# The down projection's weight split by transfers: a casting load for the high part, an adding load for the low part

## The chip, the core and the metric

The kernel runs on one core of a Trainium2 chip. The metric is device time in microseconds for one launch, the median of several runs. The engines are named as the profile names them: PE is TensorE (PEld its weight loads), DVE is VectorE, ACT is ScalarE, POOL is GpSimd and SP is SyncE; SPq, ACTq and POOLq are the queues from which they issue transfers.

## The reference, cut to what matters

One decoder layer for 256 positions of width 1024: RMSNorm, attention with 16 heads and a relative-position bias, residual, RMSNorm, a gated feed-forward network (FFN) with a causal depthwise convolution of width 3, residual, and a last RMSNorm. The change lies in the FFN, whose inner width is 2816:

```
y = rms_norm(h, ffn_norm)
u = y @ w_up                         # 256 x 1024 @ 1024 x 5632
u = causal depthwise conv of width 3 (u) + conv_b
gate, val = split(u)
h = h + (silu(gate) * val) @ w_down  # 256 x 2816 @ 2816 x 1024
out = rms_norm(h, final_norm)
```

All of it is float32.

## The kernel before

**Products from parts.** TensorE multiplies in the type fp32r, which keeps fewer bits than float32. Each operand is therefore split in two: a high part, which is the value rounded to fp32r, and a low part, which is the value less its high part. A product is the sum of three matmuls: high by high, low (activations) by high (weights), high by low.

**Splitting the weights.** Weights come from memory in loads of 1 MB into one of four `raw` tiles (`load`, L80, issued from SP's queue at L100). They are cut into units of 128 x 1024 numbers. For each unit ACT copies the raw numbers to a tile `whi` of fp32r, which rounds them (`split_hi`, L144), and DVE subtracts that from the raw numbers into a tile `wlo` (`split_lo`, L157; three units at a time of the attention part are subtracted by POOL). Behind the subtraction that ends a load's use, the next load is issued (`load_next`). There are 11 `whi` tiles and 10 `wlo` tiles in rotation.

**Order.** The list `groups` (L113 to L119) gives the order of the units, two to a group: value, query and key, output projection ("o"), and then the FFN: 22 groups "up", one for each 128 columns of the gate and the matching 128 of the value, with the 11 groups "d" of w_down (256 rows each) among them, one behind every second "up", the last three at the end (`TAIL`). `unit` (L161) makes one high part and one low part, with the high parts one unit ahead of the low parts; `split_to(g, ahead)` (L169) makes units until those of group `g` and `ahead` more are made. The program is written by hand in this order; each engine works off its own list in order.

**The FFN.** For each j of 22, `up(j)` makes 48 matmuls of 256 columns into a `bank` of PSUM; `gates(j)` (L645) evacuates it on DVE (`u`, L649), makes the convolution on ACT and DVE (`cv`, L653 to L665), the SiLU on ACT (`sl`, L672) and, one j late, the gated product and its high and low parts `at` (L656 to L668), with two calls of `unit` between these steps. Then units are split ahead, 6 or (from j = 8) 8 units beyond group j (L702). After every second j from 3 on, `down(i)` (L674) adds two units' products to four accumulators: for each unit four high matmuls of 512 columns and two low ones for each half of the positions (`rows_product`, L309). The last three groups are multiplied at the end, the first 128 positions first, and each half of the positions is normalised and stored by `finish` (L727): a power on POOL (L732), the scaling on DVE and ACT from `xg` to `o` (L737, L739), and the stores.

The start of the FFN has one more power on POOL, that of the second RMSNorm (`rstds`, L240), and the load of the last norm's weights, `gf` (L618), is issued from POOL's queue.

Of the kernel before, what the change touches and what calls it, by code (L numbers as in the profile page):

```python
# [8 lines left out]
F32 = mybir.dt.float32  # L9
F32R = mybir.dt.float32r  # L10
BF16 = mybir.dt.bfloat16
AF = mybir.ActivationFunctionType
ALU = mybir.AluOpType

P = 128
S = 256
NT = S // P
D = 1024
# [13 lines left out]
UNITS = 10  # L32
RAWS = 4
AHEAD = 6
WARM = 6
MORE_WARM = 2

# [10 lines left out]
def tile_block(ctx: ExitStack, tc, x, attn_norm, w_qkv, w_o, rel_bias, ffn_norm, w_up, conv_w,  # L48
               conv_b, w_down, final_norm, out):
    nc = tc.nc  # L50
# [3 lines left out]
    wraw = ctx.enter_context(tc.tile_pool(name="wraw", bufs=RAWS))  # L54
    wsp = ctx.enter_context(tc.tile_pool(name="wsp", bufs=UNITS))
# [21 lines left out]
    wq, wo, wu, wd = w_qkv[0], w_o[0], w_up[0], w_down[0]  # L77
# [25 lines left out]
    def parts(g):  # L103

        kind, i = g
        if kind in ("v", "o", "d"):
            t = raws[kind, i].rearrange("p (k c) -> p k c", k=2)
            return [t[:, 0, :], t[:, 1, :]]
        pair = ("qc", "kc") if kind == "qk" else ("gc", "uc")
        j = i % 2  # L110
        return [raws[n, i // 2].rearrange("p (k c) -> p k c", k=KD)[:, :, j * P:(j + 1) * P] for n in pair]

    groups = [("v", i) for i in range(4)] + [("qk", p) for p in range(NP)] + [("o", i) for i in range(4)]  # L113
# [5 lines left out]
    groups += [("d", i) for i in range(first_tail, NG)]  # L119
    order = []  # L120
    for kind, i in groups:
        if kind in ("v", "o", "d"):
            order.append((kind, i))
        elif i % 2 == 0:
            order += [(n, i // 2) for n in (("qc", "kc") if kind == "qk" else ("gc", "uc"))]
    place = {g: n for n, g in enumerate(groups)}
    hi, lo = {}, {}
    state = {"hi": 0, "lo": 0, "load": 0, "by": nc.vector}

    def load_next():  # L130
        if state["load"] < len(order):
            load(order[state["load"]])
            state["load"] += 1

    def split_hi():
        n, u = divmod(state["hi"], 2)
        if n >= len(groups):
            return
        state["hi"] += 1
        g = groups[n]  # L140
        src = parts(g)[u]
        hi[g, u] = wsp.tile([P, 1024], F32R, name="whi", bufs=UNITS + 1)
        h = hi[g, u].rearrange("p (k c) -> p k c", k=KD) if len(src.shape) == 3 else hi[g, u]
        nc.scalar.activation(h, src, AF.Copy)  # L144

    def split_lo():
        n, u = divmod(state["lo"], 2)
        if state["lo"] == state["hi"]:
            return
        state["lo"] += 1  # L150
        g = groups[n]
        src = parts(g)[u]
        lo[g, u] = wsp.tile([P, 1024], F32R, name="wlo", bufs=UNITS)
        h, l = hi[g, u].bitcast(F32), lo[g, u]
        if len(src.shape) == 3:
            h, l = (a.rearrange("p (k c) -> p k c", k=KD) for a in (h, l))
        state["by"].tensor_tensor(l, src, h, op=ALU.subtract)  # L157
        if u if g[0] in ("v", "o", "d") else g[1] % 2:
            load_next()

    def unit(count=1):  # L161

        for _ in range(count):
            if state["hi"] == state["lo"]:
                split_hi()
            split_hi()
            split_lo()

    def split_to(g, ahead=0):  # L169
        n = 2 * (place[g] + 1) + ahead  # L170
        unit(max(0, n - state["lo"]))
# [30 lines left out]
    for name, src in (("g2", ffn_norm[0]), ("b", conv_b[0]), ("w0", conv_w[0, 0]), ("w1", conv_w[0, 1]),  # L202
                      ("w2", conv_w[0, 2])):
        i, r = ROWS[name]
        n = src.shape[0] // P
# [11 lines left out]
    def first_params():  # L217
        ps = bank()
        nc.tensor.transpose(ps[:, :KD], row1, ident[:KD, :KD])
        nc.scalar.activation(g1, ps[:, :KD], AF.Copy, scale=math.sqrt(D))  # L220
# [56 lines left out]
    def keep_warm(n):  # L277
        for _ in range(n):
            mm(warm[:, :P], ones, ones, True, True)

    keep_warm(WARM)
    first_params()
# [5 lines left out]
    while d1 >= 0:  # L288
# [4 lines left out]
        n = d1 - d0 + 1  # L293
# [38 lines left out]
    g = ("v", 0)  # L332
# [37 lines left out]
    for i in range(4):  # L370
# [4 lines left out]
        for kk in range(2):  # L375
            k = 2 * i + kk
# [237 lines left out]


    fp = ctx.enter_context(tc.tile_pool(name="fp", bufs=1))
    gf = fp.tile([P, D], F32, name="gf")
    nc.gpsimd.dma_start(gf, bass.AP(tensor=final_norm.tensor, offset=final_norm.offset, ap=[[0, P], [1, D]]))  # L618
    at = {}
# [3 lines left out]
    def taps(col):  # L623
        return tuple(params[:, i, r + col:r + col + 1] for i, r in (ROWS[n] for n in ("w0", "w1", "w2", "b")))
# [12 lines left out]
    def up(j):  # L637
        split_to(("up", j))
        ps = up_ps()
        up_k(j, ps, range(KD))  # L640
        gates(j, ps)
# [3 lines left out]
    def gates(j, ps):  # L645

        if j < NF:
            u = fp.tile([P, 2, S], F32, name="u", bufs=2)
            nc.vector.tensor_tensor(u, ps, rb2.unsqueeze(1).to_broadcast([P, 2, S]), op=ALU.mult)  # L649
            c = cv[j] = fp.tile([P, 2, S], F32, name="cv", bufs=2)  # L650
            for a in range(2):
                w0, w1, w2, b = taps(a * NF + j)
                nc.scalar.activation(c[:, a, :], u[:, a, :], AF.Identity, scale=w2, bias=b)  # L653
        if j > 0:
            s = sl[j - 1]
            nc.vector.tensor_tensor(s, s, cv[j - 1][:, 1, :], op=ALU.mult)  # L656
            at[j - 1] = fp.tile([P, 2, S], F32R, name="at", bufs=10)
            nc.scalar.activation(at[j - 1][:, 0, :], s, AF.Copy)
        unit()
        if j < NF:  # L660
            for a in range(2):
                w0, w1, w2, b = taps(a * NF + j)
                nc.vector.scalar_tensor_tensor(c[:, a, 1:], u[:, a, :S - 1], w1, c[:, a, 1:],  # L663
                                               op0=ALU.mult, op1=ALU.add)
                nc.vector.scalar_tensor_tensor(c[:, a, 2:], u[:, a, :S - 2], w0, c[:, a, 2:],  # L665
                                               op0=ALU.mult, op1=ALU.add)
        if j > 0:
            nc.vector.tensor_tensor(at[j - 1][:, 1, :], s, at[j - 1][:, 0, :].bitcast(F32), op=ALU.subtract)  # L668
        unit()
        if j < NF:  # L670
            sl[j] = fp.tile([P, S], F32, name="sl", bufs=2)
            nc.scalar.activation(sl[j], c[:, 0, :], AF.Silu)  # L672

    def down(i, chains, whole=False):  # L674
        split_to(("d", i))
        for c in chains:
            if c not in accs:
                accs[c] = acc()
        for kk in range(2):
            k = 2 * i + kk  # L680
            rows_product(accs, at[k], ("d", i), kk, chains, k == 0,
                         k == NF - 1 or (CHAINS[3] if whole and kk else False), kk == 1 and chains == CHAINS)
# [12 lines left out]
    for j in range(NF):  # L695
        if j < 2:
            gates(j, first[j])
        else:
            up(j)
        if j == 4:  # L700
            nc.scalar.activation(gf, gf, AF.Copy, scale=math.sqrt(D))
        split_to(("up", j), AHEAD if j < 8 else AHEAD + 2)  # L702
        i = (j - 3) // 2
        if j >= 3 and j % 2 == 1 and i < first_tail:
            down(i, CHAINS, i == first_tail - 1)
            split_to(("d", i), AHEAD if j < 8 else AHEAD + 2)

    gates(NF, None)

    xg = [fp.tile([P, D], F32, name=f"xg{t}") for t in range(NT)]
    ends = {t: fp.tile([P, 4], F32, name=f"ends{t}") for t in range(NT)}

    def weighted(t, c, y):
        nc.vector.tensor_tensor(xg[t][:, c], y, gf[:, c], op=ALU.mult)

    def square(t, c, n, y):
        nc.scalar.activation(junk[t][:, c], y, AF.Square, accum_out=ends[t][:, n:n + 1])  # L719
# [7 lines left out]
    def finish(t, n):  # L727

        square(t, LAST[t], n, last[t])
        r = small.tile([P, 1], F32, name="rf")  # L730
        nc.vector.scalar_tensor_tensor(r, ends[t][:, n:n + 1], D * EPS, ends[t][:, 3:4], op0=ALU.add, op1=ALU.add)  # L731
        nc.gpsimd.tensor_tensor(r, r, minus_half, op=ALU.pow)  # L732
        weighted(t, LAST[t], last[t])
        o = fp.tile([P, D], F32, name="o", bufs=2)
        rows = out[0, t * P:(t + 1) * P, :]
        for c in QUARTERS:
            nc.vector.tensor_scalar(o[:, c], xg[t][:, c], r, None, op0=ALU.mult)  # L737
            nc.sync.dma_start(rows[:, c], o[:, c])
        nc.scalar.activation(o[:, :512], xg[t][:, :512], AF.Copy, scale=r)  # L739
        nc.scalar.dma_start(rows[:, :512], o[:, :512])  # L740
# [18 lines left out]
    down(NG - 1, [(0, 1)])  # L759
    last[0] = add_part(0, right, accs[0, 1])  # L760
    finish(0, 0)
    for i in range(first_tail, NG):
        down(i, [(1, 0)])
# [43 lines left out]
```

## Time and profile before

| what | value |
|---|---|
| median of 3 runs | 298.86 us (298.61 to 301.47) |
| the profiled execution's span, first to last instruction | 298.1 us |
| outside the span (median less span) | 0.8 us |
| busy in the span: PE, DVE, ACT, POOL | 290.8, 229.1, 170.4, 35.1 us |
| granted clock of PE, mean | 0.998 |
| moved by transfers | 62.07 MB, mean 208 GB/s |
| of it from POOL's queue (q0, software) | 2.65 MB |
| the FFN on PE, first full up product to the last chain's end | about 120 to 292 us |

How to read it: the engines run beside each other, so their busy times don't add up to the span; what counts is which engine the others wait for, and that is read from the waits and from the chain that ended last. A group's row gives line, engine and operation, output and inputs with shapes, count, then busy time and the mean of one in ns, then the idle time of the engine just before. In the timeline each row has start, length and what ran; the bracket at its end is the idle time before it and what ended that. "us to landing" of a transfer runs from its issue until all of it has arrived.

### The profile page before, as it was taken

The numbers are of one execution on the slowest core, as the hardware profiler recorded it, in microseconds if no ns is written. First come the engines' busy times: TensorE is split into PE (matmuls) and PEld (weight loads), VectorE is DVE, ScalarE is ACT, GpSimd is POOL, SyncE is SP. The second block draws the span as 40 slices with busy tenths as digits, with TensorE's granted clock in tenths as the row PEclk, the third lists the DMA queues.
The fourth block names the chain that finished last, engine by engine and source line by source line (L and its number), as shares of the span: only waits on it lengthen the run. The fifth ranks groups of instructions, "written<-read, shape, count | busy, mean of one in ns | idle before, by whom it ended". The sixth has DMA issues, their size and how long they took to land.

```text
span 298.1 us, 5455 instructions
## 1 busy us (share of the span) xinstructions
PE 290.8 (98%) x2112; PEld 268.7 (90%) x2112; DVE 229.1 (77%) x426; ACT 170.4 (57%) x309; POOL 35.1 (12%) x61
## 2 busy tenths in 40 slices
PE   8999999999999999999999999999999999999992
PEld 7888999979978789998989899999989898999882
DVE  3864978479588586899895959998795959599752
ACT  4684749149165676477582727766474727275341
POOL 4605008319100003000000000000000000000010
PEclk9999999999999999999999999999999999999999
DMA  7999497698796964364938191976364747400011
GB/s 243 417 384 342 155 329 211 177 412 214 253 370 166 324 214 152 125 237 144 343 122 303 44 354 49 324 224 244 132 216 136 257 143 281 144 0 2 0 70 70
DMA packets 44245, 62.07 MB, mean 208 GB/s; under 512 B 1772, under 2 KB 37308, under 8 KB 44220
## 3 DMA queue, kind: packets, MB, share of 16 engines
q1 hardware_dynamic: 42492, 58.17, 57.8%
q0 software_dynamic: 848, 2.65, 2.7%
q10 hardware_dynamic: 880, 0.92, 1.1%
q8 instruction: 16, 0.26, 0.4%
q14 instruction: 9, 0.07, 0.1%
HBM read 57.90 MB, written 3.83 MB: 207 GB/s over the span
## 4 chain that ended last, share of the span: by engine, by line
PE 86%; DMA 5%; DVE 3%; issue 3%; ACT 0%; SPq 0%; POOL 0%; POOLq 0%; DVEq 0%
PE bank L73 41%; PE acc L73 37%; PE spare L73 5%; DMA raw<-in_w_o_dram 3%; DMA weights<-turned 1%; DMA turned<-weights 1%; DVE weights L477 1%; DVE weights L475 1%; PE bank L254 1%; PE acc L254 1%; DVE xs L724 0%; DVE wlo L157 0%; SPq L482 0%; POOL rf L732 0%; ACT junk L719 0%
## 5 line engine op out<-in xcount | busy, mean ns | idle before, releaser
L73 PE MATMUL bank<-yt,whi 128*128 128x256 f32 x704 | 120.6, 277 | 0.0
L157 DVE TENSOR_TENSOR wlo<-raw,whi 128x1024 fp32r<-128x1024 f32 x90 | 107.2, 1219 | 2.0 <-ACT whi L144 1.1
L73 PEld LDWEIGHTS bank<-yt,whi 128*128 128x128 f32 x704 | 106.2, 188 | 0.0
L144 ACT ACTIVATE whi<-raw 128x1024 fp32r<-128x1024 f32 x96 | 95.3, 1047 | 9.7 <-DMA raw<-in_w_qkv_dram 6.0
L73 PE MATMUL bank<-yt,wlo 128*128 128x256 f32 x352 | 97.2, 276 | 0.0
L73 PEld LDWEIGHTS bank<-yt,wlo 128*128 128x128 f32 x352 | 66.1, 188 | 0.0
L653 ACT ACTIVATE cv<-u,params 128x256 f32<-128x256 f32 x44 | 24.1, 594 | 65.5 <-DVE u L649 65.5
L73 PE MATMUL acc<-whi,at 128*128 128x512 f32 x164 | 44.8, 390 | 0.0
L73 PEld LDWEIGHTS acc<-whi,at 128*128 128x128 f32 x164 | 30.1, 188 | 5.8
L649 DVE TENSOR_TENSOR u<-bank,rb 128x512 f32<-128x512 f32 x22 | 15.2, 691 | 21.1 <-PE bank L73 21.1
L73 PE MATMUL acc<-yt,whi 128*128 128x256 f32 x160 | 27.8, 278 | 0.0
L73 PE MATMUL acc<-wlo,at 128*128 128x512 f32 (+1 forms) x90 | 26.1, 370 | 0.0
L73 PEld LDWEIGHTS acc<-yt,whi 128*128 128x128 f32 x160 | 24.2, 188 | 0.0
L665 DVE SCALAR_TENSOR_TENSOR cv<-u,params,cv 128x254 f32<-128x254 f32 x44 | 21.3, 483 | 1.6
L73 PE MATMUL acc<-yt,wlo 128*128 128x256 f32 x80 | 22.2, 278 | 0.0
L732 POOL TENSOR_TENSOR rf<-rf,minus_half 128x1 f32<-128x1 f32 x2 | 1.5, 740 | 172.4 <-DVE rf L731 172.4
L663 DVE SCALAR_TENSOR_TENSOR cv<-u,params,cv 128x255 f32<-128x255 f32 x44 | 21.0, 478 | 0.3 <-ACT cv L653 0.3
L73 PE MATMUL acc<-whi,ot 128*128 128x512 f32 x64 | 20.1, 396 | 0.0
L73 PEld LDWEIGHTS acc<-wlo,at 128*128 128x128 f32 x90 | 16.9, 188 | 3.5
L73 PE MATMUL acc<-whi,yt 128*128 128x512 f32 x64 | 17.9, 404 | 0.0
L464 ACT ACTIVATE weights<-weights,nz 128x128 f32<-128x128 f32 (+1 forms) x32 | 14.1, 442 | 5.6 <-DVE nz L460 5.6
L73 PE MATMUL spare<-yt,whi 128*128 128x256 f32 x96 | 17.0, 281 | 0.0
(118 smaller groups left out, 334.5 us busy)
## 6 DMA issues: line engine op xcount, KB each, us to landing
raw<-in_w_up_dram SPq DMA_DIRECT2D x22, 1024.0 KB, 5.2
raw<-in_w_down_dram SPq DMA_DIRECT2D x11, 1024.0 KB, 6.4
raw<-in_w_qkv_dram SPq DMA_DIRECT2D x10, 1024.0 KB, 8.5
raw<-in_w_o_dram SPq DMA_DIRECT2D x4, 1024.0 KB, 6.7
weights<-turned SPq DMA_DIRECT2D x7, 384.0 KB, 3.8
turned<-weights SPq DMA_DIRECT2D x24, 96.0 KB, 2.0
raw<-in_w_qkv_dram SPq DMA_DIRECT2D x4, 512.0 KB, 7.6
bias<-line_d POOLq DMA_DIRECT2D x8, 256.0 KB, 4.1
```

The costliest lines, as they stand in the source:

```text
L73: nc.tensor.matmul(o, lhsT, rhs, start=start, stop=stop, skip_group_check=True)
L144: nc.scalar.activation(h, src, AF.Copy)
L157: state["by"].tensor_tensor(l, src, h, op=ALU.subtract)
L254: nc.tensor.transpose(ps[:, a, t * P:(t + 1) * P], xt[t][:, (k + a) * P:(k + a + 1) * P], ident)
L464: nc.scalar.activation(sc[p][:, a, c], sc[p][:, a, c], AF.Exp, bias=nm[:, j], accum_out=z[:, j])
L475: nc.vector.tensor_tensor(w, w, rz[:, :, t:t + 1].to_broadcast([P, 2, c.stop - c.start]), op=ALU.mult)
L477: nc.vector.transpose(blocks.rearrange("p (J g i) -> p g J i", J=4, g=6), sc[p].rearrange("p a (c J i) -> p (a c) J i", c=3, J=4))
L649: nc.vector.tensor_tensor(u, ps, rb2.unsqueeze(1).to_broadcast([P, 2, S]), op=ALU.mult)
L653: nc.scalar.activation(c[:, a, :], u[:, a, :], AF.Identity, scale=w2, bias=b)
L663: nc.vector.scalar_tensor_tensor(c[:, a, 1:], u[:, a, :S - 1], w1, c[:, a, 1:], op0=ALU.mult, op1=ALU.add)
L665: nc.vector.scalar_tensor_tensor(c[:, a, 2:], u[:, a, :S - 2], w0, c[:, a, 2:], op0=ALU.mult, op1=ALU.add)
L732: nc.gpsimd.tensor_tensor(r, r, minus_half, op=ALU.pow)
```

## The change

The 22 units of w_down are no longer loaded as raw numbers.

- Their high parts come from a transfer from memory straight into a tile `dhi` of type fp32r, issued from POOL's queue; the transfer casts. `cast_ahead` issues it, up to five units (`CASTS`) ahead of the unit whose high part is next, once the FFN's pool is open. There are six `dhi` tiles (`DOWNS`).
- In the place of the ACT copy, ACT writes the negative of the high part to the unit's `wlo` tile.
- In the place of the DVE subtraction, POOL's queue issues a second transfer of the same rows of w_down, which adds them onto that tile (`accum_op=ALU.add`).
- w_down is left out of the list of SP's loads, so the four `raw` tiles are used for w_up alone in the FFN.
- To make room, `at` has 8 tiles and not 10, and `xg` and `o` of the last steps are the two halves of `raw` tiles.

```diff
+CASTS = 5
+DOWNS = 6
...
     for kind, i in groups:
-        if kind in ("v", "o", "d"):
+        if kind == "d":
+            continue
+        if kind in ("v", "o"):
             order.append((kind, i))
...
-    state = {"hi": 0, "lo": 0, "load": 0, "by": nc.vector}
+    state = {"hi": 0, "lo": 0, "load": 0, "cast": 0, "pool": None, "by": nc.vector}
+
+    def down_rows(g, u):
+        k = 2 * g[1] + u
+        return wd[k * P:(k + 1) * P, :]
+
+    def cast_ahead():
+
+        while state["pool"] is not None and state["cast"] < min(state["hi"] + CASTS, 2 * len(groups)):
+            n, u = divmod(state["cast"], 2)
+            state["cast"] += 1
+            g = groups[n]
+            if g[0] == "d":
+                hi[g, u] = state["pool"].tile([P, 1024], F32R, name="dhi", bufs=DOWNS)
+                nc.gpsimd.dma_start(hi[g, u], down_rows(g, u))
...
         n, u = divmod(state["hi"], 2)
         if n >= len(groups):
             return
+        g = groups[n]
+        cast_ahead()
         state["hi"] += 1
-        g = groups[n]
+        if g[0] == "d":
+            lo[g, u] = wsp.tile([P, 1024], F32R, name="wlo", bufs=UNITS)
+            nc.scalar.activation(lo[g, u], hi[g, u].bitcast(F32), AF.Copy, scale=-1.0)
+            return
...
         state["lo"] += 1
         g = groups[n]
+        if g[0] == "d":
+            nc.gpsimd.dma_start(lo[g, u], down_rows(g, u), accum_op=ALU.add)
+            return
...
     fp = ctx.enter_context(tc.tile_pool(name="fp", bufs=1))
+    state["pool"] = fp
...
-            at[j - 1] = fp.tile([P, 2, S], F32R, name="at", bufs=10)
+            at[j - 1] = fp.tile([P, 2, S], F32R, name="at", bufs=8)
...
-    xg = [fp.tile([P, D], F32, name=f"xg{t}") for t in range(NT)]
+    ends_of = [wraw.tile([P, 2048], F32, name="raw") for _ in range(NT)]
+    xg = [t[:, :D] for t in ends_of]
...
-        o = fp.tile([P, D], F32, name="o", bufs=2)
+        o = ends_of[t][:, D:]
```

How the order moves, at the two places that the prediction speaks of. First ACT at the beginning of the FFN, from the first of its rows at which a unit of w_down is split; a row is the line, the operation, output and input with the tile's number, and the size. Before:

```order
L144 ACTIVATE whi_1719<-raw_1551 128x1024
L144 ACTIVATE whi_1730<-raw_1561 128x1024
L672 ACTIVATE sl_1736<-cv_1713 128x256
L144 ACTIVATE whi_1767<-raw_1561 128x1024
L144 ACTIVATE whi_1771<-raw_1586 128x1024
L653 ACTIVATE cv_1828<-u_1826,params_118 128x256 x2
```

After (line numbers of the changed kernel):

```order
L167 ACTIVATE whi_1723<-raw_1350 128x1024
L162 ACTIVATE wlo_1734<-dhi_1585 128x1024
L699 ACTIVATE sl_1740<-cv_1717 128x256
L162 ACTIVATE wlo_1771<-dhi_1649 128x1024
L167 ACTIVATE whi_1776<-raw_1555 128x1024
L680 ACTIVATE cv_1830<-u_1828,params_118 128x256 x2
```

These are the units of group ("d", 1) (`raw_1561` before). Each negation stands where the copy stood; its input is now a `dhi` tile and its output a `wlo` tile.

Second, POOL's list behind the second RMSNorm's power. Before, nothing stood there up to the end of the kernel:

```order
L618 DMA gf_1407<-in_final_norm_dram 128x1024
L240 TENSOR_TENSOR rstd_1503<-rstd_1503,minus_half_116 128x2
L732 TENSOR_TENSOR rf_3398<-rf_3398,minus_half_116 128x1
L732 TENSOR_TENSOR rf_3470<-rf_3470,minus_half_116 128x1
```

After, the first of the 44 transfers that now stand between the powers:

```order
L266 TENSOR_TENSOR rstd_1503<-rstd_1503,minus_half_116 128x2
L146 DMA dhi_1509<-in_w_down_dram 128x1024
L146 DMA dhi_1511<-in_w_down_dram 128x1024
L176 DMA wlo_1561<-in_w_down_dram 128x1024
L146 DMA dhi_1585<-in_w_down_dram 128x1024
L176 DMA wlo_1577<-in_w_down_dram 128x1024
L146 DMA dhi_1649<-in_w_down_dram 128x1024
L176 DMA wlo_1734<-in_w_down_dram 128x1024
L146 DMA dhi_1774<-in_w_down_dram 128x1024
```

The rows of L146 are casting transfers and those of L176 adding ones; the casts of a group stand behind the adds of the group before it, tile by tile, and each add waits there for ACT's negation.

## Prediction

> **What bounds the kernel now.** I read the page's engine totals first, then who TensorE waited for, then the chain that ended last, then the stretches.
>
> ```profile
> PE 290.8 (98%) x2112; PEld 268.7 (90%) x2112; DVE 229.1 (77%) x426; ACT 170.4 (57%) x309; POOL 35.1 (12%) x61
> ```
>
> ```profile
> PE spare L73 <- DVE ones L199: 1.0, 1, 1.0
> PE spare L73 <- DMA weights<-turned: 0.4, 1, 0.4
> ```
>
> ```profile
> 120.42 13.64 PE bank L73 x120
> 134.07 5.46 PE acc L73 x25
> 139.53 10.90 PE bank L73 x96
> 150.43 5.46 PE acc L73 x25
> ...
> 254.05 21.78 PE bank L73 x192
> 275.83 6.83 PE acc L73 x30
> ...
> 293.76 0.72 ACT o L739
> ```
>
> ```profile
> core 0: us, PE busy (x) PEld busy (x) DVE busy (x) ACT busy (x) POOL busy (x), PEclk, DMA share, GB/s
> 140.00:260.00 120.00, 120.00 (x897) 113.62 (x897) 97.92 (x148) 69.19 (x105) 0.00 (x0) 1.00 0.62 210
> ```
>
> The second fence is all that TensorE (PE) ever waited for: 1.4 us, none of it in the part that is changed. The chain (start, length, what) is PE alone from 120.42 to 282.66: the FFN is a period of 10.90 us of up products and 5.46 us of down products, 16.36 us together, with no gap, and in the 120 us window PE is busy 120.00 at a granted clock of 1.00. VectorE (DVE) has 22 us to spare there, ACT 51 us. The matmuls stay: same shapes, same count. So the stage is worth what PE does in it, and the edit can only leave it alone or make PE wait.
>
> **What is removed.** For w_down's 22 tiles, the DVE subtractions go, and the ACT copies become ACT negations in the same places.
>
> ```profile
> L157 DVE TENSOR_TENSOR wlo<-raw,whi 128x1024 fp32r<-128x1024 f32 x90 | 107.2, 1219 | 2.0 <-ACT whi L144 1.1
> L144 ACT ACTIVATE whi<-raw 128x1024 fp32r<-128x1024 f32 x96 | 95.3, 1047 | 9.7 <-DMA raw<-in_w_qkv_dram 6.0
> ```
>
> DVE: 22 x 1.219 = 26.8 us of work less. What hides it is PE: nothing on PE waits for DVE there, so it is worth 0. ACT: 22 copies of 1.047 us out, 22 negations of the same tile size and engine in; 0. Eleven 1 MB loads leave SP's queue; w_up then has all four `raw` tiles to itself, so its loads go out earlier; 0. At the end `xg` and `o` lie in `raw` tiles whose last readers, splits of w_up, are long done when they are written; 0, and 0 too for the last steps (L716 to L740), which keep their order.
>
> **What is added: 44 transfers of 512 KB from POOL's queue.** This trace has neither a casting nor an adding transfer. The nearest rows:
>
> ```profile
> raw<-in_w_up_dram SPq DMA_DIRECT2D x22, 1024.0 KB, 5.2
> raw<-in_w_down_dram SPq DMA_DIRECT2D x11, 1024.0 KB, 6.4
> gf<-in_final_norm_dram POOLq DMA_DIRECT2D x1, 512.0 KB, 4.9
> ```
>
> `gf` has the cast's bytes, its row length (4 KB a partition) and its queue: 4.9 us from issue to landing. I take that for a cast alone; below it I see no reason to go, and the upper end is twice it, 9.8. The window above moves 210 GB/s at a share of 0.62, so full engines move 210/0.62 = 339 GB/s, and 512 KB (0.52 MB) occupies them 1.55 us; the other 3.35 us of `gf` are fixed. An adding transfer has to read what stands in the tile as well as what comes. Lower end: `gf`'s 4.9. Upper end: two such transfers, one behind the other, 9.8. I take the bytes twice with the fixed part once, 3.35 + 3.1 = 6.5 us, as w_up's row shows that doubled bytes (1 MB) land in 5.2, far nearer 4.9 than 9.8.
>
> The Trainium skill (Collectives: The Full Stack, "The bandwidth ceiling: the fold count and why AG ≠ RS ≠ AR") says that an add inside the transfer engines is slow because of its two source reads and not because of the addition, a measured factor of 1.93 between reduce and copy. No run here shows that yet; by it the moved part would be 1.55 x 1.93 = 3.0 us, an estimate from that page, and the sum below would stay as it is.
>
> POOL itself: `gf`'s issue took 0.57 us, so 44 issues are about 25 us of an engine with nothing else in the FFN.
>
> ```profile
> 111.44 0.57 POOL L618 DMA_DIRECT2D gf<-in_final_norm_dram  x1 [35.94 <-PE acc L73]
> 117.04 2.76 POOL L240 TENSOR_TENSOR rstd<-rstd,minus_half 128x2 f32<-128x2 f32 x1 [5.04 <-DVE rstd L239]
> ```
>
> **Is any of it late?** Each tile is now a chain: cast, ACT's negation, add, PE. Start with group 0, the first, whose cast stands right behind the power at 117.04 and so leaves at 119.80.
>
> ```profile
> 121.65 1.09 ACT L653 ACTIVATE cv<-u,params 128x256 f32<-128x256 f32 x2 [3.22 <-DVE u L649]
> 122.65 1.99 ACT L144 ACTIVATE whi<-raw 128x1024 fp32r<-128x1024 f32 x2
> 124.55 0.40 ACT L672 ACTIVATE sl<-cv 128x256 f32<-128x256 f32 x1
> 126.34 1.09 ACT L653 ACTIVATE cv<-u,params 128x256 f32<-128x256 f32 x2 [1.40 <-DVE u L649]
> 127.34 0.40 ACT L658 ACTIVATE at<-sl 128x256 fp32r<-128x256 f32 x1
> 127.65 1.99 ACT L144 ACTIVATE whi<-raw 128x1024 fp32r<-128x1024 f32 x2
> ...
> 138.39 1.99 ACT L144 ACTIVATE whi<-raw 128x1024 fp32r<-128x1024 f32 x2
> 140.29 0.40 ACT L672 ACTIVATE sl<-cv 128x256 f32<-128x256 f32 x1
> 140.59 2.00 ACT L144 ACTIVATE whi<-raw 128x1024 fp32r<-128x1024 f32 x2
> ```
>
> ```profile
> L73 PE MATMUL acc<-wlo,at x90: 277/389/389, 134.8 to 287.7; 128*128 128x512 f32 x74, 128*128 128x256 f32 x16
> ```
>
> By the order of ACT the negation of group 0's first tile is the second half of the pair at 122.65: it could start at 123.65, but its cast lands at 119.80 + 4.9 = 124.7. ACT stands still 1.05 us; queued behind it are the SiLU `sl` at 124.55 and `cv` at 126.34, and the 1.40 us that ACT idled before 126.34 cover it. If the cast took the 9.8, ACT would be 6 us late and `cv`, `at` and PE's next evacuation with it. The negation ends at 125.7, and PE first reads a low part of w_down at 134.8 (first start in the row above). So the first add has 134.8 - 125.7 = **9.1 us** against 6.5. The second tile's negation is the first half of the pair at 127.65, ends 128.7, and PE wants it half a down later, 134.8 + 2.73 = 137.5: **8.8 us**.
>
> Here the engines have company. From 125.7 on, before the second add can be complete, they move the first add (1.05 MB read), the next cast that stands between the two adds in POOL's queue (0.52), the second add (1.05) and the load that SP issues at about that time (1.05): 3.67 MB. At 339 GB/s that is 10.8 us, with the fixed 3.35 it lands at 139.9, **2.3 us late**. At the 426 GB/s that the row below (105 to 140 us in 40 slices) reaches, 8.6 us and 137.7, **0.2 us late**; with adds that read once, 2.62 MB, 7.7 us and 136.8, in time. The bounds are 0 and 2.3; I take **0.5**, near the row with the fuller engines.
>
> ```profile
> GB/s 8 0 37 243 407 421 328 362 378 423 327 47 33 0 0 0 0 0 19 0 0 84 277 382 376 248 417 426 187 0 0 178 362 372 281 25 0 0 0 35
> ```
>
> Group 1: negations end at 140.4 and 141.6 (second of the pair at 138.39, first of that at 140.59), PE wants them 0.75 into the down product as before (134.8 against 134.07), at 151.2, and half a down later at 153.9: 10.8 and 12.3 us. From j = 8 on the splits run two units further ahead, so the later ones have more. The last tile, group 10:
>
> ```profile
> 272.46 1.05 ACT L144 ACTIVATE whi<-raw 128x1024 fp32r<-128x1024 f32 x1
> ```
>
> Its negation ends at 273.5; PE's chain reads it last in the piece that ends at 282.66, one 0.23 us matmul (6.83/30) earlier, 282.4: **8.9 us**, with no load beside it. 6.5 fits; 0. Its cast waits for PE to be done with the tile six before it, group 7's, about 254.05: 18 us ahead of its negation; 0.
>
> Engines over a period of 16.36 us: w_up 2.10 MB, casts 1.05, adds 2.10 read: 5.25 MB at 339 GB/s = 15.5 us. Tight, but under the period.
>
> **Sum.** 298.1 span + 0.8 around it (the median 298.86 less the span) + 0 for the work removed + 0.5 at group 0 = 299.4 us.
>
> **Rivals.** *Adds that land late at the two ends (chance 0.19).* PE waits from 9.1 us issue to landing at group 0 and from 8.9 at the last tile; all between have 10.8 or more. For it: SP's loads and both kinds of POOL's transfers share the engines at group 0. Against: the last tile is alone. An add of 12 us costs 2.9 + 3.1 = 6.0 us: 304.9.
>
> The Trainium skill (DMA: Bandwidth & Descriptors, "Queues, rings and completion order") has each engine take turns between the queues that have work. What it would do here belongs to this rival: with SP's load beside it the add's 3.1 us become 6.2 and it lands in 9.6 instead of 9.1, a wait of half a microsecond; no row here separates two queues.
>
> *The transfer engines become the bound (0.16).* If the adding or the casting moves a third of the rate, adds count 3.15 MB: 6.30 MB a period, 18.6 us, 2.2 us over PE's 16.36. Eight periods: 18 us, 317. For it: nothing in the trace prices an add. Against: it takes three times the price of the same bytes.
>
> *A gain (0.03, of it 0.02 over 1%).* DVE's 26.8 us free a place where PE waits for it. Against: PE's waits above are 1.4 us in all. Even all of it would give 297.5.
>
> **Chances.** 0.62 for the forecast: PE never or hardly waits. About 1% (3 us) is what a measurement of this kernel can tell from no change; the two late cases lie beyond it, 0.35. Faster 0.02, within 1% 0.63. The range begins at 298.2, since nothing on PE is taken away, and reaches to 311, through the first rival and short of the second; the forecast's own is 298.2 to 301.8.
>
> **What would show it.** Right: PE still has its pairs of 10.90 and 5.46 us without gaps, DVE's L157 group falls from 90 to 68, and the adds land under 9 us. Wrong: waits of PE on `wlo` transfers, first at about 135 and last before 283; or, if the engines are full, w_up's landing well over 5.2 us, ACT waiting for `raw` or `dhi` and a DMA share near 1.

## The result and the profile after

The changed kernel takes 301.24 us (median of 15 runs, 300.2 to 302.2), the kernel before, on the same chip, 299.08 us (15 runs): a ratio of 1.0053, with a 95% interval of 1.0039 to 1.0068. By the ratio that is 1.6 us more (the means of the runs lie 1.5 us apart, the medians 2.2), inside the 1% within which the forecast lay, and the sign is clear. The profiled execution has a span of 299.6 us where that of before had 298.1.

First the engine totals of the changed kernel and its groups for the new work (line numbers are those of the changed kernel, 2 to 28 higher than before):

```profile
PE 289.7 (97%) x2112; PEld 267.6 (89%) x2112; DVE 205.7 (69%) x404; ACT 170.5 (57%) x309; POOL 67.4 (22%) x105
...
L183 DVE TENSOR_TENSOR wlo<-raw,whi 128x1024 fp32r<-128x1024 f32 x68 | 81.7, 1220 | 4.6 <-ACT whi L167 3.5
L176 POOL DMA_DIRECT2D wlo<-in_w_down_dram x22 | 19.7, 894 | 111.6 <-ACT sl L699 70.2
L162 ACT ACTIVATE wlo<-dhi 128x1024 fp32r<-128x1024 f32 x22 | 22.8, 1046 | 1.4 <-DMA dhi<-in_w_down_dram 1.4
L146 POOL DMA_DIRECT2D dhi<-in_w_down_dram x22 | 17.3, 838 | 14.7 <-PE acc L75 14.7
```

DVE is 23.4 us less busy (229.1 to 205.7) and PE does the same work. The 22 negations cost ACT what the copies did (1046 ns against 1047). So the work moved as planned, and the time grew.

Who PE waited for in the changed kernel (in all, times, longest):

```profile
PE acc L75 <- DMA wlo<-in_w_down_dram: 1.3, 1, 1.3
PE spare L75 <- DVE ones L225: 1.0, 1, 1.0
PE acc L75 <- DVE whi L366: 0.8, 1, 0.8
```

Only the first wait is new in the FFN; the other two lie at the kernel's start. The chain that ended last (start, length, what) shows where it stands:

```profile
113.66 5.46 PE bank L75 x48
...
127.91 9.94 DMA wlo<-in_w_down_dram
137.84 0.04 issue
137.89 2.12 PE acc L75 x9
140.00 10.90 PE bank L75 x96
150.90 5.46 PE acc L75 x25
...
276.30 6.83 PE acc L75 x30
...
294.23 0.72 ACT raw L767
```

One add, issued at 127.91 and landed 9.94 us later, is on the chain; it is the second of group 0, and behind it the pairs of 10.90 and 5.46 us run without a gap. From the first up product (113.66) to the end of the piece of 6.83 us it is 169.47 us; before, from 114.75 to 282.66, it was 167.91: **1.56 us more, all at group 0**. (The FFN starts at another time in each execution, 113.4 to 115.5 us in the profiles of this study, because the attention part in front of it, which no kernel here changes, varies; so stages are compared by their length.)

The second half of the cost stands behind the last product. From the start of ACT's last scaling to the end of the span it is 299.6 - 294.23 = 5.4 us; before, 298.1 - 293.76 = 4.3. The instructions that close the program, before and after (count, ns min/median/max, first and last start; SP's first drain stands behind its waits for the stores):

```profile
L803 SPq EVENT_SEMAPHORE  x11: 17/28/28, 295.0 to 298.1; - x11
L803 POOLq DRAIN  x3: 46/93/1582, 293.1 to 297.9; - x3
L803 SPq DRAIN  x3: 7/7/7, 297.3 to 297.6; - x3
```

```profile
L831 SPq EVENT_SEMAPHORE  x11: 17/28/28, 295.5 to 299.5; - x11
L831 POOLq DRAIN  x3: 46/98/5172, 293.6 to 299.3; - x3
L831 SPq DRAIN  x3: 7/7/7, 297.9 to 299.0; - x3
```

POOL's first drain starts together with its last power, at 293.1 and 293.6, so that some 0.6 us of its time is the power's. It took 1.58 us and was over at 294.7, long before the stores (297.3); now it takes 5.17 us and is over at 298.8, behind the stores (297.9), and the last barrier waits for it. That adds **1.0 us**, and nothing in the prediction spoke of it. In these two profiles 1.56 and 1.0 us, less the 1.1 us by which this execution's FFN started earlier (113.66 against 114.75), are the 1.5 us between the spans.

Transfers (landing is the median from issue; q0 is POOL's queue, with packets, MB and share), and the same stretch as before:

```profile
q1 hardware_dynamic: 39500, 46.63, 47.7%
q0 software_dynamic: 7184, 25.72, 34.0%
...
raw<-in_w_up_dram SPq DMA_DIRECT2D x22, 1024.0 KB, 13.4
dhi<-in_w_down_dram POOLq DMA_DIRECT2D x22, 512.0 KB, 9.2
wlo<-in_w_down_dram POOLq DMA_DIRECT2D x22, 512.0 KB, 7.4
```

```profile
140.00:260.00 120.00, 120.00 (x898) 113.62 (x897) 80.84 (x130) 68.00 (x103) 21.60 (x31) 1.00 0.92 259
```

The share rose from 0.62 to 0.92 and w_up's loads land in 13.4 us where they took 5.2, yet PE is busy 120.00 of 120 us: all of that is hidden.

### The profile page after: what moved, and what is told of

It is laid out like the page before. It is cut to its first block, busy times and chain, and to the rows that moved or that the text cites. A ratio compares the mean times of both kernels' runs of the same rounds, so it can differ in the third digit from the quotient of the medians.

```text
span 299.6 us, 5492 instructions
## 1 busy us (share of the span) xinstructions
PE 289.7 (97%) x2112; PEld 267.6 (89%) x2112; DVE 205.7 (69%) x404; ACT 170.5 (57%) x309; POOL 67.4 (22%) x105
## 4 chain that ended last, share of the span: by engine, by line
PE 86%; DMA 5%; issue 3%; DVE 2%; ACT 1%; POOL 0%; POOLq 0%; SPq 0%
PE acc L75 41%; PE bank L75 37%; PE spare L75 7%; DMA wlo<-in_w_down_dram 3%; DMA raw<-in_w_qkv_dram 1%; PE acc L280 1%; DVE u L676 0%; DVE xs L752 0%; PE bank L280 0%; DVE wlo L183 0%; ACT cv L680 0%; DVE cv L692 0%; ACT wlo L162 0%; POOL rf L760 0%; DVE cv L690 0%
## 5 line engine op out<-in xcount | busy, mean ns | idle before, releaser
L183 DVE TENSOR_TENSOR wlo<-raw,whi 128x1024 fp32r<-128x1024 f32 x68 | 81.7, 1220 | 4.6 <-ACT whi L167 3.5
L167 ACT ACTIVATE whi<-raw 128x1024 fp32r<-128x1024 f32 x74 | 74.3, 1048 | 10.8 <-DMA raw<-in_w_qkv_dram 7.0
L75 PE MATMUL acc<-dhi,at 128*128 128x512 f32 x164 | 44.8, 390 | 0.0
L176 POOL DMA_DIRECT2D wlo<-in_w_down_dram x22 | 19.7, 894 | 111.6 <-ACT sl L699 70.2
L75 PEld LDWEIGHTS acc<-dhi,at 128*128 128x128 f32 x164 | 30.1, 188 | 5.8
L162 ACT ACTIVATE wlo<-dhi 128x1024 fp32r<-128x1024 f32 x22 | 22.8, 1046 | 1.4 <-DMA dhi<-in_w_down_dram 1.4
L146 POOL DMA_DIRECT2D dhi<-in_w_down_dram x22 | 17.3, 838 | 14.7 <-PE acc L75 14.7
## 6 DMA issues: line engine op xcount, KB each, us to landing
raw<-in_w_up_dram SPq DMA_DIRECT2D x22, 1024.0 KB, 13.4
```

The costliest lines, as they stand in the source:

```text
L75: nc.tensor.matmul(o, lhsT, rhs, start=start, stop=stop, skip_group_check=True)
L146: nc.gpsimd.dma_start(hi[g, u], down_rows(g, u))
L162: nc.scalar.activation(lo[g, u], hi[g, u].bitcast(F32), AF.Copy, scale=-1.0)
L176: nc.gpsimd.dma_start(lo[g, u], down_rows(g, u), accum_op=ALU.add)
```

## The experiments

**Group 0 by DVE.** The first two tiles of w_down are split as before: they are back in the list of SP's loads, and each `g[0] == "d"` of the change becomes this:

```diff
-        if g[0] == "d":
+        if g[0] == "d" and g[1] > 0:
```

> The changed kernel, with group 0 of w_down (its first two tiles) split as before: a load by SP, a copy by ACT, a subtraction by DVE; the other ten groups by casting and adding transfers. Theory A (two small costs: the second add of group 0 lands 1.3 us late for PE, and POOL's drain at the end, 5.17 us against 1.58, holds the last barrier by about 1.0 us): PE waits for no wlo transfer, its FFN is as long as before (from the last transposes at about 114 to the end of the last chain), the drain stays at about 5.0 us; ratio to before 1.002 to 1.004. Rival B (the transfer engines are full all through the FFN and group 0 is only where it shows first): the wait moves to group 1, PE still waits about 1 us or more, ratio stays at 1.005. Rival C (the end is later because the stores now read raw tiles): cannot be told apart here.

Measured: ratio 1.0021 (1.0005 to 1.0037), with no wait for `wlo`. Its chain and its drain:

```profile
113.71 5.46 PE bank L75 x48
119.17 0.22 PE acc L272 x2
119.38 13.64 PE bank L75 x120
133.03 5.46 PE acc L75 x25
...
274.79 6.83 PE acc L75 x30
```

```profile
L831 POOLq DRAIN  x3: 46/97/4847, 292.1 to 297.5; - x3
```

113.71 to 281.62 is 167.91 us, the length of before to the hundredth. No wait appears at group 1, so rival B has nothing for it: what is late is late at group 0 alone. The drain has four transfers less and 0.325 us less, 81 ns each; from 11 transfers (rb, line, eight of bias, gf) and 1.58 us before to 55 and 5.17 it is 3.59/44 = 82 ns each.

**The last powers off POOL**, in the changed kernel, with group 0 by DVE on top, and in the kernel before as control:

```diff
     gates(NF, None)
+    nc.scalar.activation(junk[0][:, :1], ones[:, :1], AF.Sqrt)
...
-        nc.gpsimd.tensor_tensor(r, r, minus_half, op=ALU.pow)
+        nc.scalar.activation(r, r, AF.Sqrt)
+        nc.vector.reciprocal(r, r)
```

> The changed kernel, with the two last powers on POOL replaced by a square root on ACT (its table loaded early by a dummy) and a reciprocal on DVE, so that POOL's last instruction is the issue of the last add at about 274 and its drain runs beside PE's last products. Its control is the kernel before with the same replacement. Theory A: the drain is over before the stores are, the time from the last store to the end of the span is as in the control, and the difference to the control is the wait at group 0 alone, 1.3 to 1.6 us. Rival C (the stores from raw tiles are what is late): the difference to the control stays at about 2.5 us. Against the kernel before: ratio 1.002 to 1.005 by A.

> Both together: group 0 split as before by DVE, and the last powers off POOL. Theory A: nothing is left of the cost; within 0.5 us of the control (the kernel before with the same roots), PE waits for no wlo transfer. Rival B: 1 us or more above the control, with PE waiting at group 1. Rival C: 1 us above the control at the end.

> Control: the kernel before with the last two powers on POOL replaced by a square root on ACT and a reciprocal on DVE. Its drain of 1.58 us did not hold the end in the kernel before, so by A nothing is gained by its being early; what changes is the power itself, 0.55 us on POOL against some 0.4 us on ACT and DVE with one more handover: ratio 0.997 to 1.002. B and C expect the same.

Measured: 1.0004 (0.9976 to 1.0033), 0.9985 (0.9962 to 1.0008) and, for the control, 1.0008 (0.9985 to 1.0030). From the end of PE's last product to the end of the span it is 5.8 us in both changed kernels (291.98 to 297.8, 291.06 to 296.9) and 5.7 in the control (291.90 to 297.6), where the changed kernel with its powers on POOL has 6.7 (292.86 to 299.6) and the kernel before 5.7 (292.39 to 298.1). They too store from `raw` tiles, so rival C is out. With the root on ACT, POOL's drain of the changed kernel lies beside PE's last products: it starts at 273.3, when the last add is issued, takes 10.53 us with that add's landing (8.2 us) in it, and ends at 283.8. With both costs taken out the change is as fast as its control (0.9985 against 1.0008, the intervals overlap). In the profile of the first of the three, the wait at group 0 was small:

```profile
PE acc L75 <- DMA wlo<-in_w_down_dram: 0.2, 1, 0.2
```

The difference to the control that was expected there, 1.3 to 1.6 us, did not come (the intervals overlap): its add landed in 8.85 us and not 9.94. Its FFN is still 0.9 us longer than 167.91; 0.2 of that is the wait, and why PE's next pair was slower too (11.31 us for the up products, not 10.90) is open. The wait at group 0 is not the same in every execution.

**Adds as casts.**

```diff
-            nc.gpsimd.dma_start(lo[g, u], down_rows(g, u), accum_op=ALU.add)
+            nc.gpsimd.dma_start(lo[g, u], down_rows(g, u))
```

> The changed kernel with the adding transfers made plain casting ones: the same rows, size, queue and waits, but the tile is overwritten and nothing is added, so the low parts are left out of the result. It prices the adding alone. In the changed kernel 44 transfers of POOL's queue take 34.0% less 2.7% of 299.6 us, 93.8 us of full engines, 2.13 us each. Theory A (an add moves about twice the bytes, a cast the price of a plain load, 1.55 us): the share of POOL's queue falls to about 25%, the share in the window 140 to 260 from 0.92 to about 0.76, a transfer in the place of an add lands in 5 to 6 us (7.4 before), PE's wait at group 0 goes to 0 to 0.5 us, the drain stays at 5.2 us: ratio 1.001 to 1.004. Rival B (casting is as dear as adding, 2.1 us each): share, landing and wait stay as in the changed kernel, ratio 1.005.

Measured: 1.0033 (1.0011 to 1.0054). Its transfers and its stretch:

```profile
q0 software_dynamic: 7184, 25.72, 25.3%
...
wlo<-in_w_down_dram POOLq DMA_DIRECT2D x22, 512.0 KB, 5.1
```

```profile
140.00:260.00 120.00, 120.00 (x897) 113.62 (x897) 81.50 (x132) 67.69 (x103) 16.89 (x32) 1.00 0.79 263
```

As theory A had it. A cast occupies the engines (25.3% - 2.7%) x 299.2/44 = 1.54 us, the price of a plain load; an add (93.8 - 22 x 1.54)/22 = 2.73 us, 1.77 times as much. Its row on POOL is longer too, 0.89 us against 0.53 in the mean, but the next issue starts 0.56 us behind it (124.20 and 124.76 in the changed kernel). With the plain transfer in the add's place PE does not wait at group 0 (114.84 to 282.75, 167.91 us), and what is left of the cost is the drain, 5172 ns as in the changed kernel.

**The drain by itself**: the kernel before with 88 transfers of 2 KB.

```diff
         split_to(("up", j), AHEAD if j < 8 else AHEAD + 2)
+        for _ in range(4):
+            nc.gpsimd.dma_start(fp.tile([H, BUCKETS], F32, name="tiny", bufs=4), rel_bias)
```

> The kernel before with 88 more transfers of 2 KB from POOL's queue, four for each j of the FFN, into small tiles that nobody reads. It takes the drain by itself: so far POOL's last drain took 1.58 us with 11 transfers issued from its queue, 4.85 with 51 and 5.17 with 55, which is 82 ns for each. Theory A (the drain grows with the number of transfers, whatever their size): 1.58 + 88 x 0.082 = 8.8 us; it ends at about 301.9 where the stores were over at 297.3, so the span grows by about 4.5 us, ratio 1.013 to 1.017, with PE unchanged. Rival D (it grows with bytes or descriptors: a tiny transfer has 16 rows of 128 bytes where a tile has 128 of 4 KB): drain 1.6 to 2.5 us, ratio 1.000.

Measured: 1.015 (1.0121 to 1.0179), 303.55 us.

```profile
L805 SPq EVENT_SEMAPHORE  x11: 17/28/28, 294.0 to 301.6; - x11
L805 POOLq DRAIN  x3: 46/102/8767, 292.1 to 301.4; - x3
```

The drain took 8.77 us where 1.58 + 88 x 3.59/44 = 8.76 follows from the 82 ns for each, though a transfer is 2 KB and not 512; rival D is out. PE's FFN keeps its 167.91 us (113.70 to 281.61); 0.18 MB of transfers cost 4.5 us at the end.

**One and two more copies for each tile**, to find the limit of the transfer engines:

```diff
             nc.gpsimd.dma_start(lo[g, u], down_rows(g, u), accum_op=ALU.add)
+            for _ in range(1):
+                nc.sync.dma_start(dram.tile([P, D], F32, name="more", bufs=8), down_rows(g, u))
```

> The changed kernel with one more plain copy of 512 KB for each tile of w_down, from memory to memory, issued by SP behind the tile's add and read by nobody: two more per period of the FFN. It asks how much room the transfer engines have left, where the share stands at 0.92. If a share of 1 is the limit (at 1.55 us a copy): 15.05 + 3.1 = 18.15 us of engine work in a period of 16.36, so 1.8 us more for each of eight periods, about 14 us, 313 us, PE waiting for w_up or wlo all along. If the share has idle time in it (a packet's time counts its own waiting): under 4 us more than the changed kernel, waits at group 0 and the end only.

> The same with two more copies for each tile, four per period: 15.05 + 6.2 = 21.25 us of work in 16.36. If a share of 1 is the limit: 4.9 us a period, about 39 us, 340 us. If there is idle time in the share: well under 20 us more. Between this and the run with one copy, the slope prices a transfer in a full stage: 22 more of 1.55 us would be 34 us less what stays hidden.

Measured: with one copy 301.85, 304.36, 308.34 and 308.59 us in four runs, with two 329.96 us (ratio 1.1030, 1.0993 to 1.1068). First, with one copy more, who PE waited for, the stretch, and the last add in the chain; then, with two, PE's wait, ACT's splits of w_up with what they waited for, w_up's loads, and the stretch:

```profile
PE acc L75 <- DMA wlo<-in_w_down_dram: 1.5, 1, 1.5
```

```profile
140.00:260.00 120.00, 120.00 (x898) 113.62 (x897) 82.06 (x133) 68.54 (x105) 21.60 (x31) 1.00 1.08 340
```

```profile
272.79 10.28 DMA wlo<-in_w_down_dram
```

```profile
PE acc L75 <- DMA wlo<-in_w_down_dram: 12.3, 7, 5.3
```

```profile
L167 ACT ACTIVATE whi<-raw 128x1024 fp32r<-128x1024 f32 x74 | 74.6, 1050 | 45.5 <-DMA raw<-in_w_up_dram 34.5
```

```profile
raw<-in_w_up_dram SPq DMA_DIRECT2D x22, 1024.0 KB, 24.3
```

```profile
140.00:260.00 120.00, 112.32 (x807) 103.86 (x806) 72.42 (x119) 61.88 (x92) 19.62 (x28) 0.97 1.06 337
```

The profiled execution with one copy, the fastest of the four, ran the stretch at a share of 1.08 and 340 GB/s without a wait of PE, so a share of 1 is not the limit. It and the next fit the second expectation, under 4 us more than the changed kernel's 301.24. The other two, 7 us more at a granted clock of 0.995 (0.996 and 0.997 in the first two), fit neither; they have no profile, and what they waited for stays open. In the profile group 0 is in time and the wait is at the last tile: its add, issued at 272.79, landed after 10.28 us and was 1.5 late, so 8.8 us were allowed from the issue, 9.1 from the negation's end (the prediction had 8.9).

With two copies the moved bytes no longer grow (337 GB/s), w_up's loads land in 24.3 us, ACT waits 34.5 us for them, they are 26% of the chain that ended last, PE waits in the stretch, and the kernel takes 29 us longer than the changed one. So there is a load at which transfers bound the FFN, somewhere above that of this change. Whether it is the engines that are full is not shown: the copies stand in SP's queue among w_up's loads, and no run issued them from another.

**Casts alone.** `split_hi` keeps the cast and writes no negative; SP loads the rows too (its list of loads is as before), and DVE subtracts as before:

```diff
-            lo[g, u] = wsp.tile([P, 1024], F32R, name="wlo", bufs=UNITS)
-            nc.scalar.activation(lo[g, u], hi[g, u].bitcast(F32), AF.Copy, scale=-1.0)
             return
...
-        if g[0] == "d":
-            nc.gpsimd.dma_start(lo[g, u], down_rows(g, u), accum_op=ALU.add)
-            return
```

> One half of the change alone: the high parts come from casting transfers as in the changed kernel, but the rows are loaded by SP as well, and DVE subtracts the high part from them as before; no adds, no negations on ACT. The bytes from memory are those of the changed kernel. Theory A, with what the runs have shown so far (82 ns of drain for each transfer of POOL's queue, a cast at the price of a plain load): 33 transfers from POOL's queue, drain 1.58 + 22 x 0.082 = 3.4 us, which is over before the stores are, so it costs nothing; PE waits for no transfer; ratio 0.999 to 1.002. Rival B (full engines cost time by themselves, by 2 times w_down's bytes): ratio 1.004 or more with waits of PE or ACT on transfers in the FFN.

Measured: 0.9988 (0.9955 to 1.0020), the FFN 167.91 us (114.32 to 282.23), and

```profile
L824 POOLq DRAIN  x3: 46/93/3374, 292.7 to 297.4; - x3
```

The drain is the expected 3.4 us, over at 296.1, before the stores. The bytes are those of the changed kernel, and nothing is slower: reading w_down twice costs nothing here. Its transfers give a cast's price again: 14.0% of 297.7 us less 2.7% of 298.1, by 22, is 1.53 us.

**CASTS 4**, alone and with the roots:

```diff
-CASTS = 5
+CASTS = 4
```

> The changed kernel with CASTS 4 and not 5, which moves one row in POOL's list at group 0: the cast of the next group no longer stands between its two adds but behind both. Theory A (the second add of group 0 was late by the transfers in front of it in its own queue, of which this cast is one, 0.52 MB or 1.54 us): it lands in about 8.4 us where it took 9.9, PE's wait of 1.3 us falls to 0 to 0.3 us; the drain stays at 5.17 us and holds the end by 1.0: ratio 1.002 to 1.004. Rival (the order in POOL's queue does not matter, since SP's loads and not the cast are what the add shares the engines with): the wait stays at 1 us or more, ratio 1.005.

> The changed kernel with CASTS 4 and with the last powers as a root on ACT and a reciprocal on DVE, so that POOL's drain is off the end. If the two costs are all there is, this is the whole change at no cost: ratio to the kernel before 0.998 to 1.002, as the kernel before with the same roots (1.0008) and the kernel with group 0 by DVE (0.9985). If something else is left: 1.003 or more.

Measured: 1.0030 (1.0003 to 1.0057) and 1.0015 (0.9985 to 1.0045). POOL's rows at group 0 and the chain, with CASTS 4:

```profile
124.44 0.89 POOL L176 DMA_DIRECT2D wlo<-in_w_down_dram  x1 [6.08 <-ACT sl L699]
127.61 0.88 POOL L176 DMA_DIRECT2D wlo<-in_w_down_dram  x1 [2.28 <-ACT wlo L162]
128.16 1.45 POOL L146 DMA_DIRECT2D dhi<-in_w_down_dram  x2
```

```profile
113.36 5.46 PE bank L75 x48
...
274.44 6.83 PE acc L75 x30
```

The two adds now follow each other with no cast between them, the second lands in 7.8 us where it took 9.94 (8.4 were expected), PE has no wait for `wlo`, and the FFN takes 167.91 us (113.36 to 281.27). The drain is 5172 ns as before. This fits theory A; since the wait differs from execution to execution, and the interval overlaps that of the changed kernel, the profile carries it and not the ratio. No version here beats the kernel before by more than its interval: with both costs removed the change is worth nothing, as nothing waits for what it frees.

## Why the prediction was right, point by point

- **PE bounds the FFN, and the matmuls stay.** Right. In every kernel whose adds were in time, the FFN took 167.91 us, with 22 subtractions more on DVE or without; DVE's group fell from 107.2 to 81.7 us.
- **The price of a cast and of an add.** Right in kind. A cast was taken at a plain load's 1.55 us of full engines and measured 1.54; an add at 3.1, measured 2.73. Landing alone was put at 4.9 and 6.5 us; the quickest were 3.7 and 5.4, the medians, in company, 9.2 and 7.4. The Trainium skill (Collectives: The Full Stack, "The bandwidth ceiling: the fold count and why AG ≠ RS ≠ AR") puts an add's price down to its two reads, with a measured 1.93. These runs have 1.77, near it and below it (2.73 us where the estimate from that page was 3.0). A cast costs what a plain load does.
- **Engines over a period: 15.5 of 16.36 us.** Right in what it was for: that is a share of 0.95, the window shows 0.92, and PE did not wait. But 1 is not the limit that it was held against; the run with one copy more shows 1.08.
- **Group 0: 0 to 2.3 us late, 0.5 taken.** The place, the tile and the reason were right: the second add, late by the transfers ahead of it, for with one of them put behind it (CASTS 4) it was in time. The 0.5 was a choice within the bounds and came out low: the profile has 1.3 us of wait and an FFN longer by 1.56, another execution (the last powers off POOL) 0.2 and 0.9. Over the runs, the three in which group 0 is in time (1.0021, 1.0030, 1.0033) leave 0.6 to 1.0 us of the 1.0053 for it, with intervals that in part overlap.
- **ACT's stand of 1.05 us at group 0's first cast.** It did not come: the power in front took 1.63 us and not 2.76, the cast left at 117.54, and ACT did not wait for it. ACT's one wait for a cast, 1.4 us, was at group 1, whose casts the prediction did not reckon; PE did not wait for it.
- **The last tile: 8.9 us allowed, 0.** Right; no wait. The run with one more copy put the limit at 9.1, counted in the same way.
- **POOL's issues: 25 us hidden.** POOL's busy time grew by 32 us (35.1 to 67.4; the rows of 17.3 and 19.7 overlap in part), and it was hidden.
- **The step that failed: "0 too for the last steps (L716 to L740), which keep their order".** They keep their order, but the program's close does not keep its length: POOL's drain grew by 82 ns for each of 44 transfers and ended behind the stores, which put the end 1.0 us later. This term was missing from the sum; it makes up, by the runs in which group 0 is in time (1.0021, 1.0030, 1.0033), 0.6 to 1.0 us of the 1.6. With it the sum would have been 299.4 + 1.0 = 300.4. So the forecast's 0.5 us was a third of what came. That PE hardly waits was reckoned; that the missing term stayed within the 1% was luck.
- **The rivals.** Late adds did come, at one end and for 1.3 us, below the 6 us of that case. Full engines did not: share 0.92, no wait in the stretch; two copies more for each tile show what a stage bound by transfers looks like. The gain did not come either.
- **The signs.** PE's pairs kept their length behind group 0 and DVE's group fell to 68, as said. But the adds landed in 5.4 to 10.6 us and not all under 9, and three signs of full engines came without their cost: w_up's loads at 13.4 us, ACT's 1.4 us for `dhi`, a share of 0.92. Only PE's waits told the cases apart.

## What to carry to other kernels

Work taken off an engine that nobody waits for is worth nothing, and the transfers that replace it have a first and a last deadline that the steady stage hides: reckon the chain from issue to use at the first group and at the last, with everything that stands ahead in the same queue. Count what a queue has issued over the whole program when its engine is among the last to finish. Before adding bytes to a stage, add its share of the transfer engines up: here the step from 0.62 to 0.92 cost nothing in the steady stage, and four copies more per period cost 29 us.

## What the runs showed of the hardware

POOL's drain at the end of the program grew by 82 ns for each transfer issued from POOL's queue, of 2 KB or of 512, even for those issued 95 us and more before it (ns by transfers: 1582 by 11, 3374 by 33, 4847 by 51, 5172 by 55, 8767 by 99). In these five it starts together with POOL's last instruction, a power of 0.55 us, and all transfers have landed. Where the last instruction was the issue of an add, the drain ended 2.1 to 2.3 us behind that add's landing (10.53, 9.82 and 9.31 us by 55, 51 and 55). What the drain does in this time is not shown. Here it was free up to about 4 us, when the stores are done.

The share of the transfer engines, which counts packets' time, went to 1.08 over 120 us without PE having to wait, and 340 GB/s were moved at it; with more copies in SP's queue the stretch stayed at 337 GB/s. A casting transfer of 512 KB occupied the engines for 1.54 us, an adding one for 2.73.
